# Five fixed W2 tiles, reloaded one by one behind their last use, and MLP transfers in program order, in a one-core hybrid encoder layer

## The chip, the cores and the metric

The kernel runs on one core of a Trainium2 chip. The metric is the device time of one execution, in microseconds (us). Before the change three runs took 802.73, 807.00 and 806.92 us; the median is 806.92 us. Engines are named as in the profile: PE (matmuls), PEld (weight loads of PE), ACT, DVE, POOL and SP. SP and POOL issue DMA transfers here: SP plain ones, POOL mostly copies and sums ("accumulating" transfers, which add what they read to what lies at the target).

## The reference

One encoder layer on 512 frames of width 1024: a mixer (attention with forgetting, and a gated recurrence), a cross attention to 256 memory tokens, and a squared-ReLU MLP with 4096 hidden columns. The change touches the MLP alone.

```python
def reference(x, mem, ...):
    h = x
    for l in range(DEPTH):                       # DEPTH = 1
        ...                                      # mixer and cross attention
        u = rmsnorm(h, norm_ff_g[l]) @ w1[l]     # (512, 1024) @ (1024, 4096)
        h = h + jnp.square(jax.nn.relu(u)) @ w2[l]   # (512, 4096) @ (4096, 1024)
    return rmsnorm(h, final_norm_g)
```

All data is float32. The kernel keeps float32 accuracy by splitting each operand into a high and a low part and adding three products (high x high, high x low, low x high).

## The kernel before

**Stages.** The MLP is cut into eight groups g of 512 hidden columns. A group has an *up* stage (`mlp_up7(g)`, x @ W1, 20 us or so) and a *down* stage (`mlp_down((g,))`, hidden @ W2). PE runs up 0, up 1, down 0, up 2, down 1, and so on to up 7, then down 6 and down 7 together. In groups 2 to 7 of the up stages, and in all down stages, the 2 x 2 block product is made of seven block products instead of eight, in the order `PRODUCTS` = "1", "5", "6", "2", "7", "3", "4". Each product needs one 512 KB *unit* of weights: a block of W1 or W2, or a sum of blocks. I write u51 for product "1" of up stage 5, and d31 for product "1" of down stage 3.

**Units.** A unit comes in as a raw float32 tile by DMA. ACT copies it to the high part (`split_of`, line 178: `whu` or `whd`), DVE subtracts to get the low part (line 182: `wlu` or `wld`), and PE reads both. The high parts lie in a pool of 4 buffers, the low parts too, so the split of a unit waits until PE is done with the unit four places earlier. Raw tiles of up units (`wru`, from `raw_tile`, loaded at line 1302) have three places: two in the pool `wrp` and one in the pool `s4`. So the fourth load waits until the first of these is split.

**The sums of W1** (`wsu`) and of the last group of W2 (`wsd`) are made in DRAM by POOL's transfers, eight for each group (`sum_jobs`). The class `Presum` emits one whenever PE has done a certain amount of work (`PACE`: every 3 us of PE work from 183 us on, every 10 us from 306 us on), and each waits for the matmul at which it was emitted.

**The chain of W2.** For down groups 0 to 6 the sums are made in SBUF from five raw tiles, which `chain_begin(g)` allocates and loads all at once (line 1334): a1 (block 00), c1 (00), a2 (01), b2 (11), b1 (10). POOL then adds block 11 to a2 (line 1335) and block 01 to c1 (line 1336), from DRAM. The product "1" splits a1; then POOL adds a2 to a1 (line 1346), and "6" splits that sum. "2" splits b1; then POOL adds a1 to b1 (line 1348), and "4" splits that. "5", "7" and "3" split c1, a2 and b2. `chain_begin(g - 1)` runs when the first unit of up stage g is prepared; three of its tiles come from the pool `s4` (12 buffers, shared with the hidden halves `hb` and others), one from `t4`, one from `q4`.

**Order.** `unit()` prepares each unit four places ahead of PE and keeps up to three raw tiles loaded or on the way. PE's order is fixed by the code. On the other engines a scheduler places the instructions, DMA issues on SP and POOL too, by its own estimate of when they become ready; each engine then runs its list strictly in that order, so an issue that waits holds up all that stand behind it. Two places matter below. On ACT, in each up stage the split of the unit "2" stands ahead of the copy `uV<-uU` (line 1420), which saves product "1" before product "6" adds to the same PSUM bank; so PE cannot start product "6" before the unit "2" has landed and is split. On SP, an issue of `chain_begin` for the tile a1 waits until line 1348's sum has read the old a1.

## Time and profile before

| what | value |
|---|---|
| median of 3 runs | 806.92 us |
| the profiled execution's own time | 807.47 us |
| its span (first to last instruction) | 805.8 us |
| PE busy, share of the span | 95% |
| DVE, ACT, POOL busy, share | 66%, 53%, 27% |
| mean granted TensorE clock | 0.977 |
| DMA moved | 140.84 MB |
| begin of up 0; of down 0; of up 5; of up 7; of the last down stage | 431.7; 477.4; 642.8; 737.4; 760.3 us |

The span is what the profile's rows add up to; the execution's own time has 1.7 us around it. A busy PE is not a PE at its peak, since the end of a matmul is modelled; where PE sits idle is told by the view of waits. The granted clock is a share of full speed: at 0.50 a matmul takes twice as long. In rows of the timeline the bracket gives the idle time of the engine before the instruction and what ended it.

### The profile page before, as it was taken

What the parts mean: (1) busy time and instruction counts of PE and PEld (TensorE: products, weight loads), DVE (VectorE), ACT (ScalarE), POOL (GpSimd) and SP (SyncE); (2) the same over time, 40 slices, a digit from 0 to 9 for tenths busy, and PEclk for the clock granted to TensorE, in tenths of its full rate; (3) what the DMA queues carried; (4) which work ended last, traced back from release to release, by engine and by line L of the source; (5) the groups of instructions that cost most, each with busy time, mean ns of one, the idle gap of its engine ahead of it and who ended that gap; (6) DMA issues with size and microseconds to landing.
All of it is one profiled execution on the core that took longest, in us unless ns stands there. A gap on an engine that the chain in (4) does not pass through costs nothing. (4 is left out here: it accounts for less than half of the span.)

```text
span 805.8 us, 11988 instructions
## 1 busy us (share of the span) xinstructions
PE 761.4 (95%) x4501; PEld 659.2 (82%) x4501; DVE 534.2 (66%) x844; ACT 428.2 (53%) x715; POOL 215.6 (27%) x301
## 2 busy tenths in 40 slices
PE   9999999999999999999999999795989979799896
PEld 6888888888889887888887888775979778698885
DVE  5648754678787555465465697474674958658697
ACT  5746535667565423444343963562735646373763
POOL 7116521523433285421241112011120100101015
PEclk9999999999999999999999999898998989899999
DMA  7542232242464699897899659769596675839522
GB/s 245 174 136 77 79 106 79 79 129 82 163 203 135 209 236 236 230 167 179 202 305 257 152 143 241 221 171 258 132 274 197 174 213 140 231 98 283 169 80 105
DMA packets 94572, 140.84 MB, mean 175 GB/s; under 512 B 5793, under 2 KB 66762, under 8 KB 94290
## 3 DMA queue, kind: packets, MB, share of 16 engines
q1 hardware_dynamic: 69586, 87.09, 33.4%
q0 software_dynamic: 24336, 51.93, 30.2%
q10 hardware_dynamic: 592, 1.05, 0.3%
q8 instruction: 35, 0.57, 0.3%
q14 instruction: 23, 0.19, 0.1%
HBM read 128.51 MB, written 33.57 MB: 201 GB/s over the span
## 5 line engine op out<-in xcount | busy, mean ns | idle before, releaser
L182 DVE TENSOR_TENSOR wlu<-wru,whu 128x1024 fp32r<-128x1024 f32 x42 | 50.9, 1225 | 55.1 <-ACT whu L178 55.1
L178 ACT ACTIVATE whu<-wru 128x1024 fp32r<-128x1024 f32 x42 | 43.5, 1050 | 69.6 <-DMA wru<-in_w_dram 46.5
L1414 PE MATMUL uU<-xs_hi,whu 128*128 128x256 f32 x96 | 32.9, 343 | 32.1 <-ACT uV L1420 28.3
L1414 PEld LDWEIGHTS uU<-xs_hi,whu 128*128 128x128 f32 x96 | 23.1, 241 | 33.5 <-ACT uV L1420 29.3
L1541 PE MATMUL U<-whd,hb 128*128 128x512 f32 x120 | 47.4, 395 | 1.7 <-DVE acc L1509 1.2
L425 POOL DMA_DIRECT2D wsu<-in_w_dram x24 | 29.3, 1239 | 68.4 <-PE xq L245 23.2
L1542 PE MATMUL U<-wld,hb 128*128 128x512 f32 x120 | 46.8, 390 | 0.0
L1543 PE MATMUL U<-whd,hb 128*128 128x512 f32 x120 | 46.8, 390 | 0.0
L987 POOL TENSOR_SCALAR bi<-nF,Ft 128x128 f32<-128x128 f32 (+3 forms) x32 | 23.3, 734 | 58.1 <-PE pt L1019 39.0
L182 DVE TENSOR_TENSOR wld<-wa,whd 128x1024 fp32r<-128x1024 f32 x21 | 25.7, 1222 | 16.2 <-ACT whd L178 16.1
L178 ACT ACTIVATE whd<-wa 128x1024 fp32r<-128x1024 f32 x21 | 22.1, 1051 | 18.4 <-DMA wa<-wa 8.9
L1415 PE MATMUL uU<-xs_lo,whu 128*128 128x256 f32 x96 | 31.7, 330 | 0.0
L1416 PE MATMUL uU<-xs_hi,wlu 128*128 128x256 f32 x96 | 31.5, 328 | 0.0
L1346 POOL DMA_DIRECT2D wa<-wa x7 | 6.4, 920 | 88.7 <-DVE wld L182 88.7
L182 DVE TENSOR_TENSOR wld<-wb,whd 128x1024 fp32r<-128x1024 f32 x21 | 26.8, 1274 | 4.5 <-ACT whd L178 4.5
L1541 PEld LDWEIGHTS U<-whd,hb 128*128 128x128 f32 x120 | 22.5, 188 | 8.5 <-issue 2.1
L1414 PE MATMUL uY<-xs_hi,whu 128*128 128x256 f32 x96 | 27.2, 283 | 0.0
L1415 PE MATMUL uY<-xs_lo,whu 128*128 128x256 f32 x96 | 27.2, 283 | 0.0
L1416 PE MATMUL uU<-x_hi,wlu 128*128 128x256 f32 x96 | 27.2, 283 | 0.0
L1415 PE MATMUL uU<-x_lo,whu 128*128 128x256 f32 x96 | 27.2, 283 | 0.0
L1416 PE MATMUL uY<-xs_hi,wlu 128*128 128x256 f32 x96 | 27.2, 283 | 0.0
L1414 PE MATMUL uU<-x_hi,whu 128*128 128x256 f32 x96 | 27.1, 283 | 0.0
(1007 smaller groups left out, 2747.7 us busy)
## 6 DMA issues: line engine op xcount, KB each, us to landing
wsu<-in_w_dram POOLq DMA_DIRECT2D x36, 512.0 KB, 7.2
wru<-wsu SPq DMA_DIRECT2D x24, 512.0 KB, 7.3
wru<-in_w_dram SPq DMA_DIRECT2D x18, 512.0 KB, 7.8
wb<-in_w_dram SPq DMA_DIRECT2D x14, 512.0 KB, 4.2
wa<-in_w_dram SPq DMA_DIRECT2D x14, 512.0 KB, 5.7
wsu<-wsu POOLq DMA_DIRECT2D x12, 512.0 KB, 5.6
wc<-in_w_dram SPq DMA_DIRECT2D x7, 512.0 KB
wc<-in_w_dram POOLq DMA_DIRECT2D x7, 512.0 KB, 9.0
```

Of the source, the lines that this page charges most:

```text
L178: ac.activation(hi, raw, AF.Copy)
L182: ve.tensor_tensor(lo, raw, f(hi), ALU.subtract)
L425: yield gp.dma_start(dst, block(g, b), accum_op=ALU.add)
L987: gp.tensor_scalar(bi[:, 0:n], fF[h][:, 0:n], -1.0, Ft[:, tb, h : h + 1], op0=ALU.mult, op1=ALU.add)
L1346: gp.dma_start(w["a1"], w["a2"], accum_op=ALU.add)
L1414: te.matmul(ps[:, i, :], whi[:, k, ws], xh[:, k, :], start=begin, stop=False, skip_group_check=True)
L1415: te.matmul(ps[:, i, :], whi[:, k, ws], xl[:, k, :], start=False, stop=False, skip_group_check=True)
L1416: at = te.matmul(ps[:, i, :], wlo[:, k, ws], xh[:, k, :], start=False, stop=k == UK - 1, skip_group_check=True)
L1541: te.matmul(ps, hi, whi[:, k, :], start=begin, stop=False, skip_group_check=True)
L1542: te.matmul(ps, hi, wlo[:, k, :], start=False, stop=False, skip_group_check=True)
L1543: at = te.matmul(ps, lo, whi[:, k, :], start=False, stop=k == 1, skip_group_check=True)
```

## The change

The five tiles of the chain are allocated once and keep their roles for all down groups. `chain_load` and `chain_add` stand behind the split that uses a tile last: c1 for the next group behind the split of "5", a2 behind "7", a1 and b2 behind "3", b1 behind "4"; the sum into c1 is issued behind the preparation of "7", that into a2 behind "4". The first group's five loads and two sums move from ahead of up 0 to its middle. All these transfers, the loads of the up units and, late in the program, the sums of `Presum` are kept in program order on their engine, in place of the scheduler's order. `PACE` is 16 us in place of 10 from 306 us of PE work on.

```diff
-PACE = (183.0, 3.0), (306.0, 10.0)
+PACE = (183.0, 3.0), (306.0, 16.0)
...
                 tc.add_manual_dep(dma.ins, self.at.ins.name, sync, reason="presum")
+                if self.spent > PACE[-1][0]:
+                    tc.keep_in_program_order(dma)
...
         def load():
             raw = raw_tile(name).rearrange("p (k n) -> p k n", k=shape[0])
-            nc.sync.dma_start(raw, src())
+            in_order(nc.sync.dma_start(raw, src()))
...
         def prep():
             while not box:
                 load_q.popleft()()
-            if key[0] == "u" and key[1] not in chain:
-                chain_begin(key[1] - 1)
...
+    in_order = tc.keep_in_program_order
+    RC = {"a1": "00", "c1": "00", "a2": "01", "b2": "11", "b1": "10"}
+    NEXT = {"5": ("c1",), "7": ("a2",), "3": ("a1", "b2"), "4": ("b1",)}
+    ADD = {"7": ("c1", "01"), "4": ("a2", "11")}
     chain = {}
...
-    def chain_begin(g):
-        chain[g + 1] = w = {}
-        for name, rc in (("a1", "00"), ("c1", "00"), ("a2", "01"), ("b2", "11"), ("b1", "10")):
...
-            nc.sync.dma_start(t, block2(g, rc))
-        gp.dma_start(w["a2"], block2(g, "11"), accum_op=ALU.add)
-        gp.dma_start(w["c1"], block2(g, "01"), accum_op=ALU.add)
+    def chain_load(g, name):
+        if g == 0:
+            chain[name] = t4("wb2") if name == "b2" else q4("wb1", F32) if name == "b1" else s4([2, S], f"w{name}")
+        in_order(nc.sync.dma_start(chain[name], block2(g, RC[name])))
+
+    def chain_add(g, name, rc):
+        in_order(gp.dma_start(chain[name], block2(g, rc), accum_op=ALU.add))
...
     def add_chain(g, name):
         def prep():
-            w = chain[g + 1]
             unit = new_parts([2, S], f"d{g}{name}")
             with ahead(PW):
-                split_of(unit[0], unit[1], w[RAW[name]])()
+                split_of(unit[0], unit[1], chain[RAW[name]])()
             if name == "1":
-                gp.dma_start(w["a1"], w["a2"], accum_op=ALU.add)
+                in_order(gp.dma_start(chain["a1"], chain["a2"], accum_op=ALU.add))
             elif name == "2":
-                gp.dma_start(w["b1"], w["a1"], accum_op=ALU.add)
+                in_order(gp.dma_start(chain["b1"], chain["a1"], accum_op=ALU.add))
+            if g + 1 < NG - 1:
+                for n in NEXT.get(name, ()):
+                    chain_load(g + 1, n)
+                if name in ADD:
+                    chain_add(g + 1, *ADD[name])
             units["d", g, name] = unit
...
-    chain_begin(0)
     ups = mlp_up_group(0)
     next(ups)
     to_tok(KC - 2)
     to_tok(KC - 1)
     next(ups)
+    for name in RC:
+        chain_load(0, name)
+    for add in ADD.values():
+        chain_add(0, *add)
```

How the lists of the engines change at three places. First SP, from the end of down 3 into up 5 (in these names the tiles of the chain end in the group that they serve before the change, `wa14` being a1 for down 4; `wru52` is the raw tile of product "2" of up 5). Before:

```order
L1334 DMA wa14_6198<-in_w2_dram 128x2x512
L1334 DMA wc14_6200<-in_w2_dram 128x2x512
L1334 DMA wa24_6202<-in_w2_dram 128x2x512
L1334 DMA wb24_6204<-in_w2_dram 128x2x512
L1334 DMA wb14_6206<-in_w2_dram 128x2x512
L1302 DMA wru53_6260<-in_w1_dram 128x4x256
L1302 DMA wru52_6214<-in_w1_dram 128x4x256
L1302 DMA wru57_6237<-wsu57_3591 128x1024
```

Now:

```order
L1331 DMA wc1_4595<-in_w2_dram 128x2x512
L1331 DMA wa2_4597<-in_w2_dram 128x2x512
L1331 DMA wa1_4593<-in_w2_dram 128x2x512
L1331 DMA wb2_4599<-in_w2_dram 128x2x512
L1331 DMA wb1_4601<-in_w2_dram 128x2x512
L1304 DMA wru52_6189<-in_w1_dram 128x4x256
L1304 DMA wru57_6213<-wsu57_3591 128x1024
L1304 DMA wru53_6236<-in_w1_dram 128x4x256
```

The load of c1 goes to the front, a1 stands behind c1 and a2 in place of ahead of them, and the raw tiles of "2", "7" and "3" come in the order in which PE uses them. Second POOL over the same stretch, up 4 to the end of down 3 (`wb13<-wa13` is the sum of a1 into b1 for down 3, the last two rows are the sums from DRAM for down 4). Before:

```order
L427 DMA wsd74_5206<-wsd76_5205 16x8192
L425 DMA wsd74_5206<-in_w2_dram 256x1x512
L1346 DMA wa13_5792<-wa23_5796 128x1024
L1348 DMA wb13_5800<-wa13_5792 128x1024
L1336 DMA wc14_6200<-in_w2_dram 128x2x512
L1335 DMA wa24_6202<-in_w2_dram 128x2x512
```

Now:

```order
L1344 DMA wa1_4593<-wa2_4597 128x1024
L425 DMA wsd75_5669<-in_w2_dram 256x1x512
L1346 DMA wb1_4601<-wa1_4593 128x1024
L1335 DMA wc1_4595<-in_w2_dram 128x2x512
L1335 DMA wa2_4597<-in_w2_dram 128x2x512
L425 DMA wsd77_5670<-in_w2_dram 256x1x512
```

The order of the four sums of the chain is the same, but sums of `Presum` for the last group, which were over by down 3, now still stand between and behind them. Third SP in up 0 and up 1 (`wr34` and `wr35` are the panels of up 0, `wr36` and `wr37` those of up 1). Before, where b2 and b1 of the first group were loaded earlier still:

```order
L1334 DMA wa10_4508<-in_w2_dram 128x2x512
L1334 DMA wc10_4510<-in_w2_dram 128x2x512
L198 DMA wr34a_4418<-in_w1_dram 128x4x256
L198 DMA wr34b_4422<-in_w1_dram 128x4x256
L1334 DMA wa20_4512<-in_w2_dram 128x2x512
L198 DMA wr35a_4522<-in_w1_dram 128x4x256
L198 DMA wr35b_4526<-in_w1_dram 128x4x256
L198 DMA wr36a_4626<-in_w1_dram 128x4x256
```

Now:

```order
L198 DMA wr35b_4514<-in_w1_dram 128x4x256
L1331 DMA wa1_4593<-in_w2_dram 128x2x512
L1331 DMA wc1_4595<-in_w2_dram 128x2x512
L1331 DMA wa2_4597<-in_w2_dram 128x2x512
L1331 DMA wb2_4599<-in_w2_dram 128x2x512
L1331 DMA wb1_4601<-in_w2_dram 128x2x512
L198 DMA wr36a_4625<-in_w1_dram 128x4x256
```

The first group's five loads now all stand between the last panel of up 0 and the first of up 1. PE's list is the same throughout, and in every up stage the split of "2" still stands ahead of the copy `uV<-uU` on ACT.

More of the change, by code (lines that the diff above doesn't have):

```diff
@@ L1318, in add_unit @@
         load_q.append(load)
-    chain = {}
-    RAW = {"1": "a1", "2": "b1", "5": "c1", "3": "b2", "6": "a1", "7": "a2", "4": "b1"}
-    def chain_begin(g):
-        chain[g + 1] = w = {}
-        for name, rc in (("a1", "00"), ("c1", "00"), ("a2", "01"), ("b2", "11"), ("b1", "10")):
-            if name == "b2":
-                t = t4(f"wb2{g}")
-            elif name == "b1":
-                t = q4(f"wb1{g}", F32)
-            else:
-                t = s4([2, S], f"w{name}{g}")
-            w[name] = t
-            nc.sync.dma_start(t, block2(g, rc))
-        gp.dma_start(w["a2"], block2(g, "11"), accum_op=ALU.add)
-        gp.dma_start(w["c1"], block2(g, "01"), accum_op=ALU.add)
+    RAW = {"1": "a1", "2": "b1", "5": "c1", "3": "b2", "6": "a1", "7": "a2", "4": "b1"}
+    in_order = tc.keep_in_program_order
+    RC = {"a1": "00", "c1": "00", "a2": "01", "b2": "11", "b1": "10"}
+    NEXT = {"5": ("c1",), "7": ("a2",), "3": ("a1", "b2"), "4": ("b1",)}
+    ADD = {"7": ("c1", "01"), "4": ("a2", "11")}
+    chain = {}
+    def chain_load(g, name):
[4 more added lines that the diff above has]
+        in_order(gp.dma_start(chain[name], block2(g, rc), accum_op=ALU.add))
     def add_chain(g, name):
         def prep():
-            w = chain[g + 1]
             unit = new_parts([2, S], f"d{g}{name}")
             with ahead(PW):
-                split_of(unit[0], unit[1], w[RAW[name]])()
+                split_of(unit[0], unit[1], chain[RAW[name]])()
             if name == "1":
-                gp.dma_start(w["a1"], w["a2"], accum_op=ALU.add)
+                in_order(gp.dma_start(chain["a1"], chain["a2"], accum_op=ALU.add))
             elif name == "2":
-                gp.dma_start(w["b1"], w["a1"], accum_op=ALU.add)
+                in_order(gp.dma_start(chain["b1"], chain["a1"], accum_op=ALU.add))
[4 more added lines that the diff above has]
+                    chain_add(g + 1, *ADD[name])
             units["d", g, name] = unit
```

## The prediction, on record before the run

> **What bounds the kernel now.** I read the page first, then the view of waits for PE, then for ACT and SP, and then the timeline of one wait.

> ```profile
> span 805.8 us, 11988 instructions
> PE 761.4 (95%) x4501; PEld 659.2 (82%) x4501; DVE 534.2 (66%) x844; ACT 428.2 (53%) x715; POOL 215.6 (27%) x301
> ...
> PE uU L1414 <- ACT uV L1420: 28.3, 5, 8.5
> PE uU L1414 <- ACT uY L1425: 3.8, 2, 2.5
> ```

> PE sets the end, and what it waits for is almost all in the up stages: 28.3 us in five waits at the start of product "6" (up 2 to 6), 3.8 us in two waits at product "7" (up 2 and 7). The view blames ACT's copy `uV`. The timeline of up 5 shows what the copy itself waited for:

> ```profile
> 642.81 0.28 PE L1414 MATMUL uU<-x_hi,whu 128*128 128x256 f32 x1
> ...
> 652.75 1.06 ACT L178 ACTIVATE whu<-wru 128x1024 fp32r<-128x1024 f32 x1 [9.11 <-DMA wru<-in_w_dram]
> 653.71 0.58 ACT L1420 ACTIVATE uV<-uU 128x512 f32<-128x512 f32 x1
> ...
> 654.34 0.58 PE L1414 MATMUL uU<-xs_hi,whu 128*128 128x256 f32 x1 [5.62 <-ACT uV L1420]
> ...
> ACT whu L178 <- DMA wru<-in_w_dram: 46.5, 6, 11.0
> ```

> ACT's list has the split of unit "2" ahead of the copy, and the split waits 9.11 us for its raw tile. The last row, of ACT's waits from 490 to 760 us, says the same of six such places, 46.5 us. With u the start of the up stage (642.81 here), PE ran out of work at 654.34 - 5.62 = 648.72, u + 5.9. Why the tile is late:

> ```profile
> 636.31 3.30 SPq L1334 DMA_DIRECT2D wb<-in_w_dram  x2
> 639.85 2.69 SPq L1302 DMA_DIRECT2D wru<-in_w_dram  x2
> ...
> 638.94 1.21 POOL L1336 DMA_DIRECT2D wc<-in_w_dram  x1 [9.80 <-DMA wc<-in_w_dram]
> 640.54 1.19 POOL L1335 DMA_DIRECT2D wa<-in_w_dram  x1 [0.39 <-issue]
> ...
> wru<-in_w_dram SPq DMA_DIRECT2D x2, 512.0 KB, 10.5
> ...
> q0 software_dynamic: 441, 0.87, 82.0%
> q1 hardware_dynamic: 417, 0.43, 26.7%
> ...
> q1 hardware_dynamic: 1023, 1.98, 94.2%
> ...
> SPq L1334 <- DMA wb<-wa: 102.6, 6, 21.6
> ```

> SP stood still for up to 21.6 us in front of the chain's five loads (last row). When they went, the tile of "2" came behind them and even behind that of "3": the second of the two issues of 639.85, at 642.2, 0.6 us after u began. It took 10.5 us and landed at 652.7. Meanwhile POOL's two sums ran: from 643 to 649 us its queue q0 held 82.0% of the DMA engines' time and SP's queue q1 26.7%, 0.43 MB in 6 us, where q1 alone moved 1.98 MB in the 6 us from 634 on (330 GB/s). From landing to PE's start are 1.7 us, so a tile that lands by u + 4.2 costs nothing.

> The waits cost more than themselves, since the granted clock is halved behind them:

> ```profile
> 506.70:511.90 5.20, 5.20 (x24) 5.20 (x25) 0.86 (x2) 1.26 (x2) 0.00 (x0) 0.50 0.99 356
> 560.10:563.10 3.00, 3.00 (x14) 3.00 (x15) 1.59 (x2) 1.08 (x2) 0.00 (x0) 0.50 1.01 328
> 604.80:610.80 6.00, 6.00 (x28) 6.00 (x29) 1.87 (x2) 2.51 (x4) 0.00 (x0) 0.50 0.76 294
> 654.40:658.60 4.20, 4.20 (x20) 4.20 (x21) 3.27 (x4) 2.92 (x4) 0.00 (x0) 0.50 0.46 138
> 701.80:706.40 4.60, 4.60 (x22) 4.60 (x22) 2.78 (x3) 1.99 (x3) 0.00 (x0) 0.50 0.33 114
> 751.60:757.60 6.00, 6.00 (x50) 6.00 (x51) 4.64 (x5) 5.03 (x8) 0.89 (x1) 1.00 0.86 231
> ...
> 604.72 0.58 PE L1414 MATMUL uU<-xs_hi,whu 128*128 128x256 f32 x1 [3.82 <-ACT uV L1420]
> ```

> PE worked 23.0 us at clock 0.50 behind the five waits (the first five rows): 11.5 us lost. The shortest wait with this effect is 3.82 us (last row); behind the 2.5 us wait at "7" in up 7 the clock stayed 1.00 (sixth row).

> Two of the down stages are also longer than the others:

> ```profile
> 524.98:545.67 20.69, 19.92 (x86) 15.54 (x85) 16.92 (x23) 13.30 (x18) 3.08 (x4) 1.00 0.63 192
> 621.93:642.81 20.88, 19.94 (x87) 15.54 (x85) 16.92 (x23) 13.30 (x18) 3.27 (x3) 1.00 0.53 151
> 718.33:737.39 19.06, 19.06 (x86) 15.77 (x85) 17.73 (x24) 12.49 (x18) 3.27 (x3) 1.00 0.66 200
> ```

> Down 1 and 3 take 1.6 and 1.8 us more than down 5. All that is to be had is thus 28.3 + 3.8 + 11.5 + 3.4 = 47.0 us.

> **The change, part by part.** No load, split or sum is added or removed; DMA bytes and PE's work are the same. What changes is when transfers start. I walk one boundary with the times of down 5 (begin d = 718.33; up 7 begins at 737.39, d + 19.1), which had no late unit:

> ```profile
> 722.04 0.86 POOL L1348 DMA_DIRECT2D wb<-wa  x1 [8.77 <-DVE wld L182]
> ...
> 725.90 1.22 DVE L182 TENSOR_TENSOR wld<-wa,whd 128x1024 fp32r<-128x1024 f32 x1
> 731.76 1.22 DVE L182 TENSOR_TENSOR wld<-wb,whd 128x1024 fp32r<-128x1024 f32 x1
> 734.69 1.22 DVE L182 TENSOR_TENSOR wlu<-wru,whu 128x1024 fp32r<-128x1024 f32 x1
> ...
> 730.50 0.46 SPq L1302 DMA_DIRECT2D wru<-in_w_dram  x1
> ...
> wb<-in_w_dram SPq DMA_DIRECT2D x14, 512.0 KB, 4.2
> wb<-wa POOLq DMA_DIRECT2D x7, 512.0 KB, 4.5
> ```

> The sum of a1 into b1 is issued at d + 3.7 and lands 4.5 us later, d + 8.2. The sum into c1 now stands right behind it on POOL, its tile long loaded; at q0's rate above (0.87 MB in 6 us, 3.6 us for 512 KB) it is through by about d + 12. The load of a2 goes behind the low split of "7" (725.90 + 1.22, d + 8.8), lands 4.2 us later at d + 13, and its sum is through by d + 13 + 1.2 + 3.6 = d + 18, 1 us before u; in up 5 that was u + 8. a1 goes at about d + 9, b2 before d + 12, b1 behind the low split of "4" (732.98, d + 14.7). The tile of "2" needs the place that the low split of "1" frees (735.91, u - 1.5); in up 4 and 7 its place is a hidden half that PE has passed, and it goes right behind b1 at u - 4.4. From u - 1.5 it takes 4.2 us, and some 0.4 for the end of a2's sum: u + 3.1, against u + 4.2 needed. So the wait at "6" goes, with 1 us in hand. That the early tile is enough, up 7 shows already: there "2" was issued at 730.50, and PE did not wait at "6".

> The 1 us is thin. In up 3, 6 and 7 a sum of `Presum` stands between those into c1 and a2; 3.6 us more put the end of a2's sum at u + 2.6, and a tile beside it moves at a quarter of its pace and lands at u + 4.2 to u + 5.5. The bounds for what stays of the 28.3 us: 0 if q0 is free, and 28.3 if the sums still stand in the tile's way at all places; by the walk it is nearer to 0: I keep 4. The clock follows the waits: 0 to 11.5, I keep 1.5, since such waits stay under 3.82 us. The waits at "7" came from the same sums (up 7's tile was issued at 738.3 beside them); a2's sum now ends before: 0 to 3.8, I keep 1. Down 1 and 3 were late since their sum of a2 into a1 ran beside a sum of `Presum`; the slower `PACE` leaves about 2.5 such sums for each pair of stages (39 us) instead of 4: 0 to 3.4, I keep 1.

> Costs. The last sums of `Presum` now come in down 5, and their units are used after 760 us: free, and 3.6 us if one were late. In-order waits on SP: behind c1's load, which waits for the split of "5", stand the first tiles of up 2, 13 us later than before and needed 25 us later still; free. Behind b1's wait stand "2", "7" and "3"; "2" is priced above, and "7" and "3" are needed 6 and 9 us later. On POOL the sum into a2 waits for its load, with one `Presum` sum and, 15 us off, the sum into a1 behind it; free. One place is worse: the first group's five loads.

> ```profile
> 422.32 0.37 SPq L198 DMA_DIRECT2D wr35b<-in_w_dram  x1
> 432.26 0.37 SPq L198 DMA_DIRECT2D wr36a<-in_w_dram  x1
> ...
> DMA packets 4920, 6.71 MB, mean 240 GB/s; under 512 B 210, under 2 KB 4306, under 8 KB 4887
> ...
> 455.62 0.39 PE L243 MATMUL u<-x_hi,wh36a 128*128 128x512 f32 x1
> ```

> They move from before 413 us (two of them far earlier) to right behind 422.32, into the stretch 418 to 446 us that already moves 6.71 MB at 240 GB/s, and ahead of up 1's first panel, which PE needs at 455.62. 2.6 MB more at 240 GB/s end at 418 + 9.3 / 0.24 = 456.8 for the panel's second half; its first half, split 1.1 us after it lands, makes PE wait 1 to 2 us. Bounds: 0 (the added loads at 330 GB/s: 454), and 5 + 3 for the clock. I take 2.

> Sum, against the profiled span: 805.8 - 47.0 + 4 + 1.5 + 1 + 1 + 2 = 768.3. The execution took 807.47, 1.7 more than its span, and the median of the runs is 0.5 below it: 768.3 + 1.7 - 0.5 = **769.5 us**.

> [...]

> **Rivals.** *The sums still hold "2" back.* If `Presum`'s sums meet the tile in every up stage, it lands at about u + 7, a wait of 2.8 us in six stages, 17; with the clock halved behind three of them (2.3 each, the mean of 11.5 over five), 7: 25 us instead of the 5.5 kept, 789 us. For it: the margin of 1 us, and q0's 82%. Against it: fewer sums for each stage. [...]

> *The loads start no earlier where it counts.* The tile of "2" hangs on the low split of "1"; if DVE is as late as in down 3 (u - 0.6), and the sums only swap places, the waits stay: 804 to 809 us. Against it: the sum into a2, at u - 2.3 in down 3, no longer waits for c1's load.

> *Slower: one list for all.* SP's list is now strict, and all tiles of an up stage stand behind b1's load, which waits for the split of "4", itself behind POOL's sum of a1 into b1. If that runs as late as in down 1 and 3 in every group and a `Presum` sum is in its way, "2" goes at u and lands at u + 10: 5.9 us of wait and 2.3 of clock in six stages (49), 1.7 in six down stages (10), and 5 at 455 us: 805.8 - 47.0 + 64 + 1.2 = 824 us. It decides from an average loss of 7.3 us for each up stage (44 / 6). For it: the lost freedom to overtake, which up 7's early tile made use of. Against it: the four loads ahead are spread over 10 us.

> **How the numbers follow.** The forecast 0.63, the first rival 0.20, no effect 0.04, slower 0.13. The forecast's own range is 759 (all 47 us go, nothing is added) to 783. The first rival with some spread reaches 795. The range is 759 to 795 and leaves out 0.17 and a little of the sides. A measurement of this kernel tells about 0.5% (4 us) from no change: faster 0.83, same 0.04, slower 0.13.

> **What would show it.** In the changed profile: PE's waits at products "6" and "7" under 10 us in total; the granted clock at 1.00 from 490 to 760 us in most windows; the raw tile of "2" issued before u and the sum into a2 before u - 4; no SP wait of 20 us with up tiles behind it that PE needs; all down stages near 19.1 us; a wait of at most 2 us near 455. I am wrong if PE still waits for `uV` in most stages (first rival), or if DVE, 17.7 of 19.1 us busy in down 5, becomes what ends PE's waits.

## The result, and the profile after

The changed kernel took 780.84 us (median of four runs, 776.75 to 788.14), the kernel before 806.32: the ratio is 0.970, 95% interval 0.962 to 0.979. That is a gain of 25 us, inside the stated range and 11 us above the forecast of 769.5. The profiled execution took 784.08 us. In a later job, beside the experiments, the same kernel took 775.44 us (four runs, 775.30 to 777.94), 0.961 of the kernel before in that job (0.957 to 0.965).

The span from the page, PE's waits from 430 us on, and waits of ACT and of SP's queue from 490 to 740 us (what waited, for what: sum in us, times, longest):

```profile
span 782.3 us, 11979 instructions
...
PE uU L1417 <- ACT uV L1423: 8.1, 4, 2.8
PE uU L1417 <- ACT uY L1428: 2.4, 2, 1.7
...
ACT whu L178 <- DMA wru<-in_w_dram: 31.4, 8, 8.6
ACT whd L178 <- DMA wa<-wa: 15.8, 5, 4.5
...
SPq L1331 <- DVE wld L182: 113.3, 23, 11.6
```

The waits at product "6" fell from 28.3 to 8.1 us and those at "7" from 3.8 to 2.4. SP no longer stands 21.6 us in front of the chain: its longest wait there is 11.6 us, and it is for a low split, as the change has it. ACT still waits 31.4 us for late raw tiles (46.5 before). One wait has grown: 15.8 us of ACT's waits, 8.9 before, are for `wa<-wa`, the sum of a2 into a1, which feeds product "6" of the down stage.

The stages from up 2 to up 7 (stretch, its length, PE's busy time, then the other engines, granted clock, DMA share, GB/s), PE right behind the waits of up 2 and up 5, and the wait of up 2 itself (rows of three of the up and two of the down stages are left out):

```profile
501.15:525.26 24.11, 21.89 (x169) 21.68 (x168) 13.93 (x16) 11.97 (x17) 1.41 (x2) 0.93 0.82 238
525.26:544.33 19.07, 19.07 (x86) 15.79 (x85) 17.78 (x24) 13.03 (x19) 4.56 (x4) 1.00 0.79 187
544.33:566.42 22.09, 20.40 (x169) 20.19 (x168) 14.02 (x16) 11.14 (x15) 2.32 (x3) 1.00 0.95 245
566.42:587.25 20.83, 19.62 (x87) 15.62 (x85) 17.43 (x24) 14.10 (x20) 4.48 (x5) 1.00 0.79 197
...
628.08:653.93 25.85, 23.03 (x169) 22.82 (x168) 14.00 (x16) 11.98 (x17) 1.43 (x2) 0.87 0.82 242
...
695.13:715.69 20.56, 19.59 (x86) 15.62 (x85) 17.38 (x24) 13.82 (x19) 4.38 (x4) 1.00 0.73 179
...
509.30:512.30 3.00, 3.00 (x15) 3.00 (x16) 3.00 (x4) 2.33 (x3) 0.00 (x0) 0.57 0.38 113
636.80:642.10 5.30, 5.29 (x25) 5.29 (x25) 3.78 (x4) 2.88 (x4) 0.00 (x0) 0.50 0.54 148
...
509.28 0.39 PE L1417 MATMUL uU<-xs_hi,whu 128*128 128x256 f32 x1 [2.22 <-ACT uV L1423]
```

The six up stages take 137.4 us together, 165.1 before: this is the gain. In up 2 and up 5 PE is busy 21.89 and 23.03 us where up 3 needs 20.40, since the clock fell behind their waits of 2.2 and 2.8 us (0.57 and 0.50 in the two rows): 1.5 + 2.6 = 4.1 us. Two of the down stages are again late (20.83 and 20.56 us, downs 2 and 5), only others than before. Up 0 and 1 need 44.4 us where they needed 45.7. Against all this, up 0 began at 437.68 us, 6.0 us later than before.

These 6 us have nothing to do with the MLP. They come from one weight panel of the cross attention, `wr27b`. The issues on SP and POOL, the split on ACT and what PE lost, in the profiled execution; then the first three in that of the later job:

```profile
310.29 1.18 POOL L425 DMA_DIRECT2D wsu<-in_w_dram  x1
311.46 0.37 SPq L198 DMA_DIRECT2D wr27b<-in_w_xq_dram  x1
319.81 1.06 ACT L178 ACTIVATE wh27b<-wr27b 128x1024 fp32r<-128x1024 f32 x1 [5.41 <-DMA wr27b<-in_w_xq_dram]
...
PE xq L243 <- ACT x_hi L1132: 2.7, 1, 2.7
...
320.00:330.00 10.00, 7.61 (x20) 5.82 (x21) 2.65 (x4) 3.13 (x4) 4.15 (x4) 0.66 0.87 171
```
```profile
310.70 0.37 SPq L198 DMA_DIRECT2D wr27b<-in_w_xq_dram  x1
311.76 1.18 POOL L425 DMA_DIRECT2D wsu<-in_w_dram  x1
315.85 1.06 ACT L178 ACTIVATE wh27b<-wr27b 128x1024 fp32r<-128x1024 f32 x1 [1.17 <-DMA wr27b<-in_w_xq_dram]
```

Where a sum of `Presum` is issued 1.2 us ahead of the load, the panel is split 8.4 us after its load's issue; where the load goes 1.1 us ahead, 5.2 us after. On ACT the instruction that makes `x_hi`, which PE needs, stands behind this split, so PE waits 2.7 us and then works at a lower clock (0.66 from 320 to 330 us, 1.00 in the profile before). The kernel is the same, so this race falls either way: in the fourteen profiles of this study the sum was first in five (the split 7.4 to 10.0 us after the load's issue), the load in nine (4.7 to 7.7 us). Up 0 began at 435.9 to 438.0 us in the five and at 430.1 to 432.2 in the nine. The race is part of the difference between 784.08 and 775.44 us, and no part of what the change does: both ways of it were met with the tiles' new roles and without them.

### The profile page after: what moved, and what is told of

Read it like the earlier page. It is cut to its first block, busy times and chain, and to the rows that moved or that the text cites. A ratio compares the mean times of both kernels' runs of the same rounds, so it can differ in the third digit from the quotient of the medians.

```text
span 782.3 us, 11979 instructions
## 1 busy us (share of the span) xinstructions
PE 756.1 (97%) x4501; PEld 654.5 (84%) x4501; DVE 533.0 (68%) x844; ACT 427.3 (55%) x715; POOL 215.5 (28%) x301
## 5 line engine op out<-in xcount | busy, mean ns | idle before, releaser
L178 ACT ACTIVATE whu<-wru 128x1024 fp32r<-128x1024 f32 x42 | 44.2, 1053 | 60.3 <-DMA wru<-in_w_dram 31.4
L182 DVE TENSOR_TENSOR wlu<-wru,whu 128x1024 fp32r<-128x1024 f32 x42 | 51.0, 1220 | 25.6 <-ACT whu L178 25.6
L1417 PE MATMUL uU<-xs_hi,whu 128*128 128x256 f32 x96 | 29.7, 310 | 10.6 <-ACT uV L1423 8.1
L182 DVE TENSOR_TENSOR wld<-wa,whd 128x1024 fp32r<-128x1024 f32 x21 | 25.6, 1221 | 17.9 <-ACT whd L178 17.8
L178 ACT ACTIVATE whd<-wa 128x1024 fp32r<-128x1024 f32 x21 | 22.1, 1054 | 20.6 <-DMA wa<-wa 15.8
L1417 PEld LDWEIGHTS uU<-xs_hi,whu 128*128 128x128 f32 x96 | 20.2, 210 | 12.0 <-ACT uV L1423 9.3
L182 DVE TENSOR_TENSOR wld<-wb,whd 128x1024 fp32r<-128x1024 f32 x21 | 26.7, 1270 | 4.5 <-ACT whd L178 3.6
L1419 PE MATMUL uU<-xs_hi,wlu 128*128 128x256 f32 x96 | 28.9, 301 | 0.0
L1418 PE MATMUL uU<-xs_lo,whu 128*128 128x256 f32 x96 | 28.9, 301 | 0.0
## 6 DMA issues: line engine op xcount, KB each, us to landing
wsu<-in_w_dram POOLq DMA_DIRECT2D x36, 512.0 KB, 6.5
wru<-wsu SPq DMA_DIRECT2D x24, 512.0 KB, 6.0
wru<-in_w_dram SPq DMA_DIRECT2D x18, 512.0 KB
wa<-in_w_dram SPq DMA_DIRECT2D x14, 512.0 KB, 7.9
wb<-in_w_dram SPq DMA_DIRECT2D x14, 512.0 KB, 6.3
wsu<-wsu POOLq DMA_DIRECT2D x12, 512.0 KB, 5.8
wc<-in_w_dram SPq DMA_DIRECT2D x7, 512.0 KB, 4.6
wc<-in_w_dram POOLq DMA_DIRECT2D x7, 512.0 KB, 7.9
```

Source lines behind the costliest of these rows:

```text
L178: ac.activation(hi, raw, AF.Copy)
L182: ve.tensor_tensor(lo, raw, f(hi), ALU.subtract)
L1417: te.matmul(ps[:, i, :], whi[:, k, ws], xh[:, k, :], start=begin, stop=False, skip_group_check=True)
L1418: te.matmul(ps[:, i, :], whi[:, k, ws], xl[:, k, :], start=False, stop=False, skip_group_check=True)
L1419: at = te.matmul(ps[:, i, :], wlo[:, k, ws], xh[:, k, :], start=False, stop=k == UK - 1, skip_group_check=True)
```

## The experiments

The theory at the start: the gain comes from the chain's loads being spread over the down stage (the fixed roles), so that the tile of "2" and the sum into a2 start earlier; what is left of the waits is the sums of POOL beside that tile. The rivals: the slower `PACE` is the gain, or the program order of the issues is. Each ratio below is to the kernel before in the same job.

| kernel | median us | ratio, 95% |
|---|---|---|
| changed, `PACE` 10 | 780.2 | 0.969 (0.964 to 0.974) |
| before, `PACE` 16 | 803.2 | 0.996 (0.993 to 1.000) |
| changed, order left to the scheduler | 780.5 | 0.968 (0.965 to 0.972) |
| before, in program order, `PACE` 16 | 801.6 | 0.996 (0.993 to 0.999) |
| changed, once more | 775.4 | 0.961 (0.957 to 0.965) |
| changed, copy ahead of the split | 775.8 | 0.961 (0.957 to 0.966) |
| changed, `PACE` 3 | 790.2 | 0.979 (0.972 to 0.985) |
| before, copy ahead of the split | 797.1 | 0.987 (0.982 to 0.992) |
| changed, sums behind "6" and "2" | 795.5 | 0.989 (0.982 to 0.995) |
| the same, copy ahead | 791.6 | 0.986 (0.977 to 0.994) |
| changed, sums behind "6" and "4" | 772.5 | 0.960 (0.957 to 0.962) |
| the same, copy ahead | 769.7 | 0.954 (0.951 to 0.957) |

### Which part of the change brings the gain

Four kernels take the three parts (roles, order, `PACE`) apart. The pace undone:

```diff
-PACE = (183.0, 3.0), (306.0, 16.0)
+PACE = (183.0, 3.0), (306.0, 10.0)
```

> The changed kernel with PACE 10 again: the last 14 sums of Presum come every 10 us of PE work in place of 16. Theory (the gain comes from the chain's loads being spread, PACE is a small term): 778 to 788 us, PE's waits at products "6" and "7" 10 to 16 us in place of 10.5. Rival (fewer sums beside the tile of "2" are the gain): over 797 us, waits over 22 us.

The pace alone, in the kernel before:

```diff
-PACE = (183.0, 3.0), (306.0, 10.0)
+PACE = (183.0, 3.0), (306.0, 16.0)
```

> The kernel before with PACE 16 alone. Theory (PACE is a small term): 800 to 810 us, PE's waits behind the copy uV 22 to 30 us. Rival (PACE is most of the gain): under 790 us, waits under 15 us.

The order undone (the line that keeps `Presum`'s late sums in order goes too):

```diff
-    in_order = tc.keep_in_program_order
+    in_order = lambda dma: dma
...
-                if self.spent > PACE[-1][0]:
-                    tc.keep_in_program_order(dma)
```

> The changed kernel without any order kept: fixed tiles, loads behind the splits and PACE 16, but the scheduler places all issues. Theory (the roles carry the gain): 776 to 790 us. Rival (the kept order carries it, without it the scheduler puts the loads late again): 797 us or more, waits behind uV over 20 us.

The order and the pace without the roles, in the kernel before (the same `in_order` around its two sums from DRAM, the sums in the chain and the late sums of `Presum`):

```diff
-            nc.sync.dma_start(raw, src())
+            in_order(nc.sync.dma_start(raw, src()))
...
-            nc.sync.dma_start(t, block2(g, rc))
+            in_order(nc.sync.dma_start(t, block2(g, rc)))
```

> The kernel before, its five loads still at once, with program order kept for the chain's transfers, the up units' loads and the late sums of Presum, and PACE 16. Theory (the order without the roles brings little, since a1's load still waits for the sum into b1 and the other four and the tile of "2" stand behind it): 798 to 815 us, SP's waits of 20 us still there. Rival (the order carries the gain): under 790 us.

PE's waits in the four, in this order:

```profile
PE uU L1417 <- ACT uV L1423: 13.1, 6, 4.1
```
```profile
PE uU L1414 <- ACT uV L1420: 20.0, 4, 7.4
PE uU L1414 <- ACT uY L1425: 7.7, 3, 4.1
```
```profile
PE uU L1415 <- ACT uV L1421: 11.6, 4, 4.2
```
```profile
PE uU L1417 <- ACT uY L1428: 15.6, 5, 6.5
PE u L243 <- ACT x_hi L1132: 5.1, 1, 5.1
PE uU L1417 <- ACT uV L1423: 3.1, 3, 2.2
```

The two kernels with the roles lie at 0.968 and 0.969, the two without at 0.996: in time the roles are the gain, and pace and order are worth 0.4% together without them. (Fixed tiles and loads spread behind the splits come together in the roles; no run parts them.) The last kernel shows the difference well. With the order kept the tile of "2" comes ahead of "3", so the wait at "6" is nearly gone, and it stands at "7" instead (15.6 us): the chain's five loads still start late, and SP's longest wait in front of them is 21.2 us:

```profile
SPq L1337 <- DMA wb<-wa: 95.0, 6, 21.2
```

Its time hides that the order does something in the up stages. In its profile up 2 to up 7 took 150.1 us together, 15 us fewer than before (137.4 in the changed kernel). But up 0 and 1 took 53.3 us, 7.7 more than before: the five loads of the first group now stand on SP right ahead of the panels `wr35a` and `wr35b` of up 0, ACT waited 5.8 and 4.7 us for these, and PE 5.1 us for the `x_hi` that ACT makes behind their splits. Another 6.2 us went ahead of up 0, where this execution had the sum first at `wr27b`. Order without the roles, but with the first group's loads moved into up 0, was not run; it might keep half of the gain.

What the order or the slower pace, each alone, adds to the roles is at most some 5 us (775.4 to 780.8 us for the whole against 780.2 and 780.5); the runs of the whole differ by as much between two jobs, so it stays open. The roles without both were not run.

> The changed kernel itself once more, as the measure for the runs beside it. The loss of 6 us at the panel wr27b near 320 us (in the profiled run, of a span of 782.3) is a race of one load against one sum: if it comes and goes, spans near 775 to 777 without it and 782 to 786 with it are seen; if it is fixed, all spans are near 782.

Its four runs lie within 2.6 us, and its profile (span 776.2) has the load of `wr27b` ahead. None of the four took 782 us or more, so the expected pair of spans is not seen in them; two other kernels of the same job (the copy ahead of the split, `PACE` 3) had the sum ahead in their profiles.

### What the waits at "6" are worth

The copy `uV<-uU` is put ahead of the split of "2" on ACT: that unit is prepared one product later, and its split gets an edge of order behind the copy.

```diff
-        while unit_q and len(order) - len(unit_q) < at + 4:
+        while unit_q and len(order) - len(unit_q) < at + (3 if key[0] == "u" and key[2] == "1" else 4):
...
-                split_of(unit[0], unit[1], box[0])()
+                copy_first(key, split_of(unit[0], unit[1], box[0])())
```

> The kernel before with the copy uV ahead of the split of "2", five loads at once and PACE 10 as they were. Theory (the late tile costs what it comes later than its own product needs it, u + 7 or so, and it lands at u + 10 to 13): 28.3 us behind uV shrink to 10 to 18 us behind the split of "2" or "7", less half clock: 778 to 792 us. Rival (the wait only moves to "2" with its full size): 800 us or more.

Both were wide of it: 797.1 us. The waits behind `uV` are gone, but little of what they cost is won:

```profile
PE uU L1414 <- ACT uY L1425: 15.5, 4, 6.1
PE uV L1414 <- ACT whu L178: 9.1, 4, 4.7
```

The late tile makes PE wait at "2" itself (9.1 us), and the tile of "7" behind it is as late. So in the kernel before, ACT's order is worth 11 of the 40 us that these waits and the clock behind them cost; the late loads are the rest.

> The changed kernel with the copy uV ahead of the split of "2" in ACT's list in all six up stages, nothing else of weight. Theory (PE waits at "6" only since the copy stands behind the late split; "2" itself is used 2.9 us later): the 8.1 us behind uV are gone, 1 to 3 us come back at "2" or "7", the half clock of up 5 goes too (2.6 us): 768 to 774 us. Rival (the wait only moves to product "2"): 777 to 784 us, with 6 us or more of waits behind wlu or whu.

No gain at all, 775.8 against 775.4 us, and yet the rival did not hold either: the waits did not move to "2". Against the profile of the same kernel without the edit, up 2 to up 7 are 9.4 us shorter together, and downs 1 to 5 are 7.3 us longer (another 3.7 us went ahead of up 0, where this profile has the sum first at `wr27b`). The windows of up 5 and down 4:

```profile
624.26:645.18 20.92, 20.40 (x170) 20.20 (x169) 14.37 (x16) 11.11 (x15) 1.43 (x2) 1.00 0.91 274
645.18:667.86 22.68, 19.92 (x87) 15.55 (x86) 17.42 (x24) 13.82 (x19) 4.26 (x4) 1.00 0.71 176
```

Up 5 is 4.9 us shorter than in the changed kernel, and down 4, which took 19.07, has grown by 3.6. Its "6" had to wait for the sum of a2 into a1, which landed 7.0 us after its issue and 0.1 us before the split (the bracket of the split names PE, which came at nearly the same time). That sum's issue on POOL and the split behind it on ACT, first in this kernel's down 4 (begin 645.18), then in the changed kernel's downs 1 and 2 (begin 525.26 and 566.42):

```profile
641.04 0.89 POOL L1344 DMA_DIRECT2D wa<-wa  x1 [4.22 <-DVE wld L182]
648.12 1.06 ACT L178 ACTIVATE whd<-wa 128x1024 fp32r<-128x1024 f32 x1 [5.45 <-PE U L1546]
```
```profile
519.32 0.88 POOL L1344 DMA_DIRECT2D wa<-wa  x1 [11.43 <-DVE wld L182]
524.23 1.06 ACT L178 ACTIVATE whd<-wa 128x1024 fp32r<-128x1024 f32 x1 [2.40 <-DMA wa<-wa]
...
561.31 0.89 POOL L1344 DMA_DIRECT2D wa<-wa  x1 [13.61 <-DVE wld L182]
567.50 1.06 ACT L178 ACTIVATE whd<-wa 128x1024 fp32r<-128x1024 f32 x1 [4.51 <-DMA wa<-wa]
```

With d the begin of the down stage, this split began at d + 2.9, d - 1.0 and d + 1.1, and the stages took 22.68, 19.07 and 20.83 us. Read off these stages, a down stage is 19.06 us, and longer by (begin of that split - d) + 0.7 where that is above zero: 19.06 + 2.9 + 0.7 = 22.7, and 19.06 + 1.1 + 0.7 = 20.9. For delays up to 3 us this line gives downs 1 to 5 of the changed kernel and of all kernels made from it to within 0.1 us, but for one stage (down 3 without the kept order, 19.7 for 19.4). Of eight delays from 5 to 7.2 us five fit as well, and three stages are 0.6 to 1.0 us longer. In the kernels without the roles the late stages are 0.5 us shorter than the line. The sum is issued 5.9 us ahead of d where all goes well, since it waits for the low split of "1", which PE's passing of an earlier unit lets begin. In down 1 above it takes 4.9 us to the split, which is 1.0 us ahead of d; the line costs from 0.7 us ahead on, so 0.3 us are in hand. A shorter up stage does not give it more. In the five stages of the run with the copy ahead the sum was issued only 3.4 to 5.6 us ahead of d, and took longer where more was under way beside it (7.1 us in down 4, issued 4.1 us ahead; a sum of `Presum` and a load of an up unit were on the way).

### The sums of `Presum`

```diff
-PACE = (183.0, 3.0), (306.0, 16.0)
+PACE = (183.0, 3.0), (306.0, 3.0)
```

> The changed kernel with PACE 3 to the end: the last 14 sums of Presum are over in up 1 and none runs in the up stages 2 to 7. Theory (Presum's sums beside the tile of "2" make most of the waits that are left): waits at "6" and "7" 10.5 us down to under 4, no half clock in up 5: 768 to 776 us. Rival (the sum into a2 and the loads of b1 and "7" beside it hold the tile, Presum does not): waits 8 to 11 us, 776 to 784 us.

Neither held. The time rose to 790.2 us, through one place:

```profile
PE U L1544 <- ACT V L1554: 9.6, 1, 9.6
PE uU L1417 <- ACT uV L1423: 7.1, 6, 1.9
...
480.54 1.41 POOL L1344 DMA_DIRECT2D wa<-wa  x1
493.17 1.06 ACT L178 ACTIVATE whd<-wa 128x1024 fp32r<-128x1024 f32 x1 [7.99 <-DMA wa<-wa]
```

The sums of `Presum` now run through up 1 and down 0. The sum of a2 into a1 was issued only 1.1 us ahead of the down stage, the split behind it came 12.6 us later, and down 0 took 39.3 us. Where no sum of `Presum` is left, from up 3 on, things go as the theory has it, but by less: up stages 3 to 6 took 20.8 to 21.8 us (21.8 to 25.9 in the changed kernel), downs 2 to 5 19.1 to 19.5 us. At "6" PE still waits 7.1 us, up to 1.9 at a time. Up stages 3 to 6 lie 1.15 us above their shortest, 20.15 (below), where they lay 2.8 us above it: `Presum` is about 60% of what is left there, and most of that is one stage: 4.3 of the 6.7 us saved are up 5's. The rest has the sum into a2 beside the tile; it was not taken away alone.

Next, the sums were placed by hand: `PACE` 10 through up 1, then two sums in each up stage and none in the down stages (the call of `presum.tick` in the down stage is replaced as the one shown).

```diff
-                presum.tick(6 * HS / 2400, at)
+                presum.at = at
...
-                ac.activation(bank["Y"], ps, AF.Copy)
+                ac.activation(bank["Y"], ps, AF.Copy), presum.emit()
             elif name == "2":
-                square(ps, qa[:, :, h1])
+                square(ps, qa[:, :, h1]), presum.emit()
```

> The changed kernel with the sums of Presum placed by hand: PACE 10 through up 1, then two sums in each up stage, behind products "6" and "2", when the tile of "2" has landed, and none in the down stages. Theory (Presum's sums beside the tile of "2" and in the down stages cost what the run without them in groups 3 to 6 saved: 1.3 us for an up stage, 0.45 for a down stage): 775.4 - 8 - 2.7 = 765 us, 761 to 769; all down stages near 19.1 us, waits at "6" under 7 us. Rival (the sum into a2 alone holds the tile, Presum does not matter): 773 to 778 us, waits as in the changed kernel.

> The same with the copy uV ahead of the split of "2" on ACT as well. Theory (the copy gave nothing before since Presum's sums made the down stages late as soon as the up stages were short): up stages near 20.5 us and down stages near 19.2 us, 757 to 763 us. Rival (ACT and DVE need the time that PE waits: what the up stages lose, the down stages take again): 763 to 771 us, down stages of 20.5 us or more.

All four expectations failed, 795.5 and 791.6 us. With the copy ahead every up stage took 20.2 us, the shortest seen, and the down stages took 22.1 to 27.6. The cause is the line above. The place behind "6" and "2" lies straight in front of the sum into a1; down 3 of the first of the two (begin 604.03):

```profile
592.97 1.04 POOL L425 DMA_DIRECT2D wsd<-in_w_dram  x1 [12.75 <-PE uU L1419]
595.85 1.04 POOL L425 DMA_DIRECT2D wsd<-in_w_dram  x1 [1.83 <-PE uV L1419]
598.13 0.91 POOL L1344 DMA_DIRECT2D wa<-wa  x1 [1.25 <-DVE wld L182]
...
610.09 1.06 ACT L178 ACTIVATE whd<-wa 128x1024 fp32r<-128x1024 f32 x1 [9.50 <-DMA wa<-wa]
```

The sum into a1 was issued in time, at d - 5.9, but with two sums ahead of it in POOL's queue it took 12 us: 19.06 + 6.1 + 0.7 = 25.8, as measured (25.79).

So one of the two was moved behind the last product "4", to the other side of the sum into a1:

```diff
-                square(ps, qa[:, :, h1]), presum.emit()
+                square(ps, qa[:, :, h1])
...
-                square(ps, qa[:, :, h2])
+                square(ps, qa[:, :, h2]), presum.emit()
```

> Presum's two sums of each up stage set apart: one behind product "6", one behind the last product "4", so that one stands ahead of the sum of a2 into a1 on POOL and one behind it. Theory (with both ahead, the sum of a2 into a1 landed up to 12 us later than in the changed kernel and "6" of the down stage waited for it; one alone is over in time): down stages 19.1 to 20 us, up stages about 21.3 us, 763 to 770 us. Rival (any sum in the up stage delays the sum into a1): down stages over 22 us, 780 us or more.

> The same with the copy uV ahead of the split of "2" on ACT. Theory: up stages 20.2 to 20.6 us as in the run with both sums ahead, down stages 19.1 to 20 us: 757 to 765 us. Rival (DVE and ACT, 17.8 of 19.1 us busy, take in the down stages what the up stages lose): down stages of 20.5 us or more, 767 to 775 us.

The first took 772.5 us, with down stages of 19.8 to 22.1 us and up stages of 21.4 in the mean: nearer to the theory, and short of it. One sum ahead is not always over in time: in down 3 it was issued 5.1 us ahead of the sum into a1, which then took 8.3 us to land. (The "12 us later" of the expectation is what the sum took in all with two ahead.) With the copy ahead it is 769.7 us (0.954) and the fastest kernel of the study: its interval ends where that of the changed kernel, against the kernel before in another job, begins (0.957). Up 2 and down 1 of it, and ACT's wait for the sum into a1:

```profile
499.32:519.48 20.16, 20.16 (x170) 20.15 (x169) 13.66 (x15) 11.34 (x15) 2.06 (x2) 1.00 0.95 258
519.48:540.97 21.49, 19.96 (x86) 15.54 (x85) 17.43 (x24) 13.82 (x19) 4.50 (x4) 1.00 0.85 187
...
ACT whd L178 <- DMA wa<-wa: 23.5, 5, 5.3
```

The up stages are at their floor. The down stages are above 20.5 us, as the rival said, but not for its reason. DVE is busy 17.4 us in them and no more than in the other kernels. In all five late ones ACT waited for the sum into a1, whose split began 1.0 to 2.5 us into the stage, and the line gives their lengths to within 0.1 us. To start that sum earlier was not tried.

## Why the prediction came out as it did

The mechanism was right: the late tile of "2" held PE through ACT's list, the spread loads bring it forward, and most of the waits go. The forecast's time was 11 us too low against the median, 6 us against the later job. By its own terms, what stays of the 47.0 us or is added:

| term | predicted us | profiled us |
|---|---|---|
| waits at "6" | 4 | 8.1 |
| half clock behind waits | 1.5 | 4.1 |
| waits at "7" | 1 | 2.4 |
| late down stages | 1 | 3.3 |
| the first panel of up 1 | 2 | 0 |
| ahead of up 0 | 0 | 6.0 |
| sum | 9.5 | 23.9 |

The right column gives 805.8 - 47.0 + 23.9 = 782.7, the span was 782.3 us.

- **The tile of "2"** was the mis-sized term. Its issue was right (u - 1.5 predicted; 626.91 in up 5, u - 1.2), its transit was not. The walk took each transfer nearly as if alone. Up 5 after the change:

```profile
618.11 0.97 SPq L1331 DMA_DIRECT2D wa<-in_w_dram  x2
621.04 3.30 SPq L1331 DMA_DIRECT2D wb<-in_w_dram  x2
626.91 0.37 SPq L1304 DMA_DIRECT2D wru<-in_w_dram  x1
...
622.86 1.21 POOL L1335 DMA_DIRECT2D wa<-in_w_dram  x1 [8.18 <-DMA wa<-in_w_dram]
623.58 1.55 POOL L425 DMA_DIRECT2D wsd<-in_w_dram  x1
...
635.22 1.06 ACT L178 ACTIVATE whu<-wru 128x1024 fp32r<-128x1024 f32 x1 [8.59 <-DMA wru<-in_w_dram]
...
wsd<-in_w_dram POOLq DMA_DIRECT2D x1, 512.0 KB, 10.7
...
wa<-in_w_dram SPq DMA_DIRECT2D x14, 512.0 KB, 7.9
```

  The tile took 8.3 us (4.2 predicted) and its split began at u + 7.1, with the load of b1 ahead of it and a sum of `Presum` of 10.7 us beside it. That is the landing of the first rival, at one place of six; at the others the split began at u + 3.6 to u + 6.0. The loads of a2 and a1 took 7.9 us in the median (last row), where the walk had 4.2 for that of a2: they go as a pair, beside the sum into c1. So the sum into a2 was issued late as well, and up 5 is still the best case: u - 5.2 there, u - 4.7 to u - 1.4 in the other five, where u - 6 was predicted. It landed at u + 1.3 to u + 7.6, not at u - 1, so the sign "before u - 4" holds at two places of six only.
- **The late down stages** hardly went (3.3 of 3.4 us), and this step of the prediction failed: it held that the sum into a1 is late beside a sum of `Presum`, and that the slower pace thins these. For the kernel before that is borne out: in the late downs 1 and 3 a sum of `Presum` had been issued 0.6 and 3.4 us ahead of it, and with `PACE` 16 alone downs 1 to 5 all took 19.1 us. In the changed kernel downs 2 and 5 are late with no sum of `Presum` under way ahead of the sum into a1 (6.1 and 6.7 us to landing), while in downs 3 and 4 one ran beside it and it took 4.6 and 4.8 us. What differs in the two late ones is a second load of an up unit: in the 4 us ahead of the sum two were issued (1.4 to 3.5 us ahead), against one (2.8 to 3.8 us ahead) in downs 1, 3 and 4. That these loads are the cause is not shown.
- **The clock**: the term assumed that waits under 3.82 us leave it alone. Waits of 2.2 and 2.8 us halved it in up 2 and up 5; what the profiles show beside that is in the last section. The 6 us from the first rival's 789 us to the upper end of the range, 795 us, are an estimate of the author's that no run shows; the half clock behind these two waits cost 1.5 and 2.6 us.
- **The costs** were overstated: PE did not wait near 455 us, and up 0 and 1 even gained 1.2 us. The strict list of SP shows no cost: the tile of "2" was issued at u - 3.1 to u - 1.0 in all six stages, where the slower rival has it at u.
- **Ahead of up 0** the race of `wr27b` was not foreseen; no view of one execution could show that it falls both ways.
- **Two slips in the working** change nothing of the forecast: the issue at 642.2 us is 0.6 us ahead of u (642.81), not after it, and the terms of the first rival, 17 and 7 us, add up to 24 us and not to 25, so that it stands at 788 us.

## What to carry to other kernels

When a late transfer is moved forward, price its transit by what will be in flight beside it at the new time, not by its best time alone: in up 5 the tile of "2" took 8.3 us, where the walk took 4.2, the median of another load. A wait that is removed helps little if the next link does not start earlier too: here the sum into a1 was, from down 1 on, issued at most 5.9 us ahead of its stage, however short or long the up stage was, and each time the up stage shrank or the queue filled, it became what PE waited for. For background transfers the place in the queue can matter more than their rate: the same sums gave 772 us or 795 us by the place of every second one. And look at where an experiment loses time, not at its total alone: the kept order without the roles seemed worth 0.4%, with 15 us won in the up stages and most of it lost elsewhere.
